# Moving the MLP's weight pieces inside longer buffers, by 16 to 448 bytes, with one raw buffer fewer

## The chip, the cores and the metric

The kernel runs on one core of one Trainium2 chip. The metric is the device time of one execution in microseconds, as the median of several runs; lower is better. The profile shows one execution on that core, with the engines TensorE (PE, its weight loads as PEld), VectorE (DVE), ScalarE (ACT), GpSimd (POOL) and the queue of SyncE (SP), which issues the transfers.

## The reference

One decoder layer on 256 tokens of width 2048, in float32. The input is normalised and multiplied by one wide matrix `w_in`; its columns feed a state-space group and an attention group with a token indexer. Their outputs are joined, multiplied by `w_out` and added to the input. Then comes the MLP, where most of the time lies:

```python
    x = x + jnp.concatenate([y_ssd, y_att], axis=-1) @ w_out      # w_out: 2048 x 2048

    u = rmsnorm(x, g_mlp) @ w_up                                  # w_up: 2048 x 8192
    return x + jnp.square(jax.nn.relu(u)) @ w_down                # w_down: 8192 x 2048
```

Every weight is read once, 204 MB in all, and every product is 256 rows high.

## The kernel before, in words

A float32 weight is split into a high part in TensorE's rounded float32 format and the rest, in the same format, and the activations likewise. A product is then three matrix multiplications: high by high, high by low, low by high. All of them add up in PSUM.

Weights come in **pieces** of 128 partitions by at most 1024 columns (4 KB a partition, 512 KB in all). The function `operands` makes one piece: SP issues its transfer into a buffer `raw` (L119), ACT copies it to `whi` with rounding (L122), DVE subtracts the two and writes `wlo` (L123). There are four buffers for `raw` (RB) and five each for `whi` and `wlo` (WB). A buffer is used again when its last reader is done: a `raw` when DVE has subtracted, a `whi` or `wlo` when TensorE is past its last matmul.

TensorE's order is written by hand. ACT's, DVE's and SP's is set by a scheduler that works with estimated times and priorities; pieces have a priority that places them 600 instructions ahead.

Two functions use pieces:

- `product` has the weights as the **moving** operand: two 512-column slices to a piece. The activations are the stationary operand, loaded 128 columns at a time (512 bytes a partition). Per slice and block of 128 rows there are three matmuls: L141 (high, high), L142 (the activations' low part), L143 (the weights' low part). The blocks of `w_in` named k, m0, m1, q0, q1, z0 and z1, the product with `w_out` and the MLP's `down` use it. The blocks m0 and m1 are 304 columns wide, the others 512.
- `product_t` has the weights as the **stationary** operand: eight 128-column slices to a piece. The moving operand is the activations, high and low side by side: 512 columns against the high weights (L181), 256 against the low ones (L182). The blocks qi and xbc of `w_in` and the MLP's `up` use it.

The MLP has four quarters q. `up(q)` makes eight units j of 256 columns of u (four pieces, 32 pairs of L181 and L182 each). `down(q)` makes four units j of 512 output columns (eight pieces, 96 matmuls each). The order is up(0), up(1), down(0), up(2), down(1), up(3), down(2), down(3). The very first unit of up(0) is multiplied ahead of the loop.

Where things stand in a partition's memory is fixed when the program is built. In bytes past a multiple of 512, the program of before has every `whi` and every `wlo` at 480 (its ten buffers are 4096 bytes apart), the activations `hx` and `x2x` at 32, and `uh`, `ul`, `yah`, `yal`, `ysh` and `ysl`, the stationary operands of `down` and of the product with `w_out`, at 224. Slices of 128 or 512 columns keep these remainders, because they are whole multiples of 512 bytes. In the blocks of 304 columns the second slice of a piece is 1216 bytes on, at 160.

Of the kernel before, what the change touches and what calls it, by code (L numbers as in the profile page):

```python
# [10 lines left out]
F32R = mybir.dt.float32r  # L11
# [5 lines left out]
P = 128  # L17
# [10 lines left out]
HP = 600  # L28
WARM = 9
WB = 5  # L30
RB = 4


Z0, XBC0, DT0, Q0, K0, V0, QI0, KI0, WI0, END = (
# [31 lines left out]
def hymba_kernel(ctx: ExitStack, tc: tile.TileContext, xn, xt, w_in, w_out, w_up, w_down, vcol, vrow, out):  # L66
# [3 lines left out]
    wts = ctx.enter_context(tc.tile_pool(name="wts", bufs=1))  # L70
# [24 lines left out]
    def step():  # L95
        for t in list(tasks):
            if isinstance(t[1], int) and t[1] > 0:
                t[1] -= 1
            elif not isinstance(t[1], str) or t[1] in done:
                advance(t)  # L100
# [6 lines left out]
        return vc[:, VC[name] + i:VC[name] + i + 1]  # L107


    def operands(src, n, load=None):  # L110

        with tc.high_priority(offset=HP):
            raw = wts.tile([P, n], F32, name="raw", tag="raw", bufs=RB)
            hi = wts.tile([P, n], F32R, name="whi", tag="whi", bufs=WB)
            lo = wts.tile([P, n], F32R, name="wlo", tag="wlo", bufs=WB)
            step = n if load is None else n // 2
            for i in range(0, n, step):
                s = slice(i, i + step)
                nc.sync.dma_start(raw[:, s], src[:, s])  # L119
                if load is not None:  # L120
                    load()
                nc.scalar.copy(hi[:, s], raw[:, s])  # L122
                nc.vector.tensor_tensor(lo[:, s], raw[:, s], hi[:, s].bitcast(F32), op=OP.subtract)  # L123
        return hi, lo

    def mp(name):
        return ps.tile([P, 512], F32, name=name, tag="mid")

    def accumulators():
        return [ps.tile([P, 512], F32, name="acc", tag="acc") for _ in range(2)]  # L130

    def product(src, n, left, load=None, tail=None):


        acc = accumulators()
        last = KT if tail is None else KT - 4

        def part(kt, out, b, wh, wl):
            s = slice(b * P, (b + 1) * P)
            ah, al = left(kt)  # L140
            nc.tensor.matmul(out, ah[:, s], wh, start=(kt == 0), stop=False)  # L141
            nc.tensor.matmul(out, al[:, s], wh, start=False, stop=False)  # L142
            nc.tensor.matmul(out, ah[:, s], wl, start=False, stop=(kt == KT - 1))  # L143

        kept = []
        halves = [(1, slice(0, n // 2)), (1, slice(n // 2, n))]
        if tail is not None:
            acc.append(mp("acc_t"))
        for kt in range(KT):
            if kt % 2 == 0:  # L150
                hi, lo = operands(src[kt // 2], 2 * n, load)
            w = slice(kt % 2 * n, kt % 2 * n + n)
            wh, wl = hi[:, w], lo[:, w]
            if kt < last:
                part(kt, acc[0][:, :n], 0, wh, wl)
                if tail is None:
                    part(kt, acc[1][:, :n], 1, wh, wl)
                else:
                    for i, (b, c) in enumerate(halves):
                        part(kt, acc[1 + i][:, c], b, wh[:, c], wl[:, c])  # L160
            else:
                kept.append((kt, wh, wl))
            step()
        if tail is not None:
            for i, (b, c) in enumerate([(0, slice(0, n))] + halves):
                for kt, wh, wl in kept:
                    part(kt, acc[i][:, c], b, wh[:, c], wl[:, c])
                tail(b, c, acc[i][:, c])
        return acc

    def product_t(src, right):

        acc = accumulators()
        for i in range(4):
            hi, lo = operands(src[i], 1024)
            c = i % 2
            for k in range(8):
                kt = 8 * (i // 2) + k
                x = right(kt)
                s = slice(k * P, (k + 1) * P)  # L180
                nc.tensor.matmul(acc[c], hi[:, s], x, start=(kt == 0), stop=False)  # L181
                nc.tensor.matmul(acc[c][:, T:], lo[:, s], x[:, :T], start=False, stop=(kt == KT - 1))  # L182
                if k % 4 == 3:
                    step()
        return acc

    def total(dst, acc):

        for c in range(2):
            nc.scalar.copy(dst[:, c, :], acc[c][:, T:])  # L190
            nc.vector.tensor_tensor(dst[:, c, :], acc[c][:, :T], dst[:, c, :], op=OP.add)
# [45 lines left out]
    for name, cols in IN_BLOCKS:  # L237
        n = sum(b - a for a, b in cols)
# [3 lines left out]
    def in_block(name, load=None):  # L242
        o, n = in_off[name]
        src = w_in[o:o + n * D].rearrange("(g p c) -> g p c", g=8, p=P)
        return product(src, n, h_left, load)

    def in_pair(name, i):
        o = in_off[name][0] + i * 256 * D
        return product_t(w_in[o:o + 256 * D].rearrange("(h p c) -> h p c", h=4, p=P), lambda kt: hx[:, kt, :])
# [436 lines left out]
    def run():  # L686
# [58 lines left out]
        for j in range(4):  # L745
            spawn(residual(j, product(w_out[j], 512, y_left)), f"res{j}")
# [4 lines left out]
    def x2(kt):  # L751
        if kt >= KT - 4:
            need("res3")
        return box[0][:, kt, :]

    first = product_t(w_up[0], x2)
    while tasks:
        step()
# [11 lines left out]
    def up(q):  # L770
        uh = mlp.tile([P, KT, T], F32R, name="uh")
        ul = mlp.tile([P, KT, T], F32R, name="ul")
        for j in range(8):
            r = mlp.tile([P, 2, T], F32, name="r")
            total(r, first if q + j == 0 else product_t(w_up[8 * q + j], x2))
            nc.vector.scalar_tensor_tensor(r, r, 0.0, r, op0=OP.max, op1=OP.mult)
            s = slice(2 * j, 2 * j + 2)
            nc.scalar.copy(uh[:, s, :], r)
            nc.vector.tensor_tensor(ul[:, s, :], r, uh[:, s, :].bitcast(F32), op=OP.subtract)
        return uh, ul  # L780

    def down(q, u):
        for j in range(4):

            def add(b, c, acc):
                c = slice(512 * j + c.start, 512 * j + c.stop)
                nc.vector.scalar_tensor_tensor(xr[:, b, c], acc, rs4[:, b:b + 1], xr[:, b, c], op0=OP.mult, op1=OP.add)
                if q == 3:
                    nc.sync.dma_start(out[b * P:(b + 1) * P, c], xr[:, b, c])

            end = q == 3 and j == 3
            acc = product(w_down[4 * q + j], 512, lambda kt: (u[0][:, kt, :], u[1][:, kt, :]), tail=add if end else None)
            for b in range(0 if end else NB):
                add(b, slice(0, 512), acc[b])

    u = [up(0)]
    for q in range(1, 4):
        u.append(up(q))
        down(q - 1, u[q - 1])
    down(3, u[3])  # L800


# [50 lines left out]
```

## Time and profile before

| | |
|---|---|
| time, median of 3 runs | 1112.91 us (1112.75 to 1113.02) |
| the profiled execution's own time | 1111.47 us |
| its span, first to last instruction | 1109.4 us |
| TensorE busy | 1100.4 us (99%) |
| TensorE's weight loads busy | 937.9 us (85%) |
| DVE busy | 692.4 us (62%) |
| ACT busy | 535.0 us (48%) |
| read from HBM | 204.29 MB, 186 GB/s over the span |

A busy TensorE is one with a matmul under way. Matmuls overlap, so the length of one says little. What counts is the distance from the start of one to the start of the next, which is read from the first and the last start in a stretch and the count between them. A wait of ACT or DVE costs something only where TensorE then waits for them.

### The profile page before, as it was taken

The numbers are of one execution on the slowest core, as the hardware profiler recorded it, in microseconds if no ns is written. First come the engines' busy times: TensorE is split into PE (matmuls) and PEld (weight loads), VectorE is DVE, ScalarE is ACT, GpSimd is POOL, SyncE is SP. The second block draws the span as 40 slices with busy tenths as digits, with TensorE's granted clock in tenths as the row PEclk, the third lists the DMA queues.
The fourth block names the chain that finished last, engine by engine and source line by source line (L and its number), as shares of the span: only waits on it lengthen the run. The fifth ranks groups of instructions, "written<-read, shape, count | busy, mean of one in ns | idle before, by whom it ended". The sixth has DMA issues, their size and how long they took to land.

```text
span 1109.4 us, 14959 instructions
## 1 busy us (share of the span) xinstructions
PE 1100.4 (99%) x5686; PEld 937.9 (85%) x5686; DVE 692.4 (62%) x976; ACT 535.0 (48%) x749; POOL 41.4 (4%) x41
## 2 busy tenths in 40 slices
PE   9999998999999999999999999999999999999998
PEld 7988887888888888888888888888888888888887
DVE  6886989667765565656565456565555565554443
ACT  7755645556765454444443334444434444333431
POOL 0010131112000000000000000000000000000000
PEclk9999999999999999999999999999999999999999
DMA  9855435644375555556656655655666556665662
GB/s 327 270 195 175 152 106 175 194 147 134 115 256 185 184 181 184 187 189 189 183 186 198 193 190 190 191 190 190 192 192 191 188 188 191 198 195 191 209 212 73
DMA packets 63735, 207.36 MB, mean 187 GB/s; under 512 B 7216, under 2 KB 11568, under 8 KB 63664
## 3 DMA queue, kind: packets, MB, share of 16 engines
q1 hardware_dynamic: 63520, 206.36, 58.1%
q8 instruction: 45, 0.74, 0.3%
q14 instruction: 26, 0.21, 0.1%
q10 hardware_dynamic: 144, 0.05, 0.0%
HBM read 204.29 MB, written 2.10 MB: 186 GB/s over the span
## 4 chain that ended last, share of the span: by engine, by line
PE 92%; DVE 4%; DMA 1%; issue 1%; ACT 1%; SPq 0%; POOL 0%; ACTq 0%; DVEq 0%
PE acc L181 27%; PE acc L141 16%; PE acc L142 16%; PE acc L143 16%; PE acc L182 14%; DVE wlo L123 1%; DVE bc L495 1%; PE ps_y L566 1%; DVE sc L459 1%; DMA xrow<-in_xn 1%; PE ps_sr L650 0%; PE ps_l L604 0%; PE ps_o L629 0%; ACT xrow L230 0%; DMA raw<-in_w_in 0%
## 5 line engine op out<-in xcount | busy, mean ns | idle before, releaser
L123 DVE TENSOR_TENSOR wlo<-raw,whi 128x1024 fp32r<-128x1024 f32 (+3 forms) x400 | 466.9, 1170 | 380.9 <-ACT whi L122 377.7
L122 ACT CAST whi<-raw 128x1024 fp32r<-128x1024 f32 (+3 forms) x400 | 400.5, 1004 | 497.4 <-PE acc L142 248.7
L181 PE MATMUL acc<-x2x,whi 128*128 128x512 f32 x1024 | 359.9, 395 | 0.0
L182 PE MATMUL acc<-x2x,wlo 128*128 128x256 f32 x1024 | 287.8, 281 | 0.0
L181 PEld LDWEIGHTS acc<-x2x,whi 128*128 128x128 f32 x1024 | 192.5, 188 | 45.4
L142 PE MATMUL acc<-whi,ul 128*128 128x512 f32 (+1 forms) x512 | 197.6, 386 | 0.0
L141 PE MATMUL acc<-whi,uh 128*128 128x512 f32 (+1 forms) x512 | 197.5, 386 | 0.0
L143 PE MATMUL acc<-wlo,uh 128*128 128x512 f32 (+1 forms) x512 | 197.5, 386 | 0.0
L182 PEld LDWEIGHTS acc<-x2x,wlo 128*128 128x128 f32 x1024 | 192.0, 188 | 0.1
L181 PE MATMUL acc<-hx,whi 128*128 128x512 f32 x320 | 114.0, 397 | 0.0
L141 PEld LDWEIGHTS acc<-whi,uh 128*128 128x128 f32 x512 | 96.1, 188 | 19.5
L143 PEld LDWEIGHTS acc<-wlo,uh 128*128 128x128 f32 x512 | 96.1, 188 | 19.5
L142 PEld LDWEIGHTS acc<-whi,ul 128*128 128x128 f32 x512 | 96.2, 188 | 19.2
L182 PE MATMUL acc<-hx,wlo 128*128 128x256 f32 x320 | 90.0, 281 | 0.0
L143 PE MATMUL acc<-wlo,hx 128*128 128x512 f32 (+1 forms) x224 | 83.0, 370 | 3.1 <-DVE wlo L123 3.1
L141 PE MATMUL acc<-whi,hx 128*128 128x512 f32 (+1 forms) x224 | 85.4, 381 | 0.1
L142 PE MATMUL acc<-whi,hx 128*128 128x512 f32 (+1 forms) x224 | 82.6, 369 | 0.0
L181 PEld LDWEIGHTS acc<-hx,whi 128*128 128x128 f32 x320 | 60.3, 188 | 13.5
L182 PEld LDWEIGHTS acc<-hx,wlo 128*128 128x128 f32 x320 | 60.1, 188 | 0.0
L143 PEld LDWEIGHTS acc<-wlo,hx 128*128 128x128 f32 x224 | 42.0, 187 | 12.0 <-DVE wlo L123 4.7
L141 PEld LDWEIGHTS acc<-whi,hx 128*128 128x128 f32 x224 | 42.2, 188 | 7.7 <-issue 0.7
L142 PEld LDWEIGHTS acc<-whi,hx 128*128 128x128 f32 x224 | 42.1, 188 | 7.4 <-issue 0.7
(224 smaller groups left out, 828.4 us busy)
## 6 DMA issues: line engine op xcount, KB each, us to landing
raw<-in_w_up SPq DMA_DIRECT2D x128, 512.0 KB, 3.7
raw<-in_w_down SPq DMA_DIRECT2D x128, 512.0 KB, 4.0
raw<-in_w_in SPq DMA_DIRECT2D x72, 512.0 KB, 3.6
raw<-in_w_out SPq DMA_DIRECT2D x32, 512.0 KB, 3.6
raw<-in_w_in SPq DMA_DIRECT2D x16, 256.0 KB, 4.2
raw<-in_w_in SPq DMA_DIRECT2D x16, 152.0 KB, 5.3
raw<-in_w_in SPq DMA_DIRECT2D x8, 304.0 KB, 2.9
xT<-in_xt SPq DMA_DIRECT2D x16, 128.0 KB, 4.1
```

The source lines that it names most:

```text
L122: nc.scalar.copy(hi[:, s], raw[:, s])
L123: nc.vector.tensor_tensor(lo[:, s], raw[:, s], hi[:, s].bitcast(F32), op=OP.subtract)
L141: nc.tensor.matmul(out, ah[:, s], wh, start=(kt == 0), stop=False)
L142: nc.tensor.matmul(out, al[:, s], wh, start=False, stop=False)
L143: nc.tensor.matmul(out, ah[:, s], wl, start=False, stop=(kt == KT - 1))
L181: nc.tensor.matmul(acc[c], hi[:, s], x, start=(kt == 0), stop=False)
L182: nc.tensor.matmul(acc[c][:, T:], lo[:, s], x[:, :T], start=False, stop=(kt == KT - 1))
L459: nc.vector.scalar_tensor_tensor(sc[:, :nk], rl[:, i, :nk], wis[:, b, h:h + 1], neg[:, T - nk:] if first else sc[:, :nk], op0=OP.mult, op1 ...
L495: nc.vector.scalar_tensor_tensor(o[:, j, :], pad[:, j, k:k + T], vcp("conv_w", 12 * k + ct), o[:, j, :], op0=OP.mult, op1=OP.add)
L566: nc.tensor.matmul(pt[:, 64 * i:64 * i + 64], m[i // 4][:, i % 4, :], xdt[:, c, 64 * h:64 * h + 64], start=True, stop=True)
```

## The change

Two things are edited. The buffers for `whi` and `wlo` get 128 more columns (512 bytes a partition), and in the MLP a piece is placed `shift` columns into its buffer. The shift comes from a table, by quarter and unit. For `up(q)`, unit j, it is entry j of row q; for `down(q)`, unit j, it is entry j + 1. All other pieces, and the first unit of up(0), are at shift 0. In bytes, the shifts of `up` are 64j for q = 0, 32j for q = 1, 16j for q = 2 and 64(7 - j) for q = 3; those of `down` are 64, 128, 192, 256 for q = 0; 32, 64, 96, 128 for q = 1; 16, 32, 48, 64 for q = 2; and 384, 320, 256, 192 for q = 3. And there are three buffers for `raw` instead of four.

A buffer is now 4608 bytes, nine times 512, and ten of them add 5120 bytes; the dropped `raw` gives back 4096. In the built program of the change `whi` and `wlo` still start at 480 past a multiple of 512 at shift 0, `x2x` still at 32, `uh` and `ul` still at 224. So the shifts are all that changes in these remainders.

```diff
-RB = 4
+RB = 3
+SPARE = 128
+
+
+SHIFTS = [[16 * j for j in range(8)], [8 * j for j in range(8)], [4 * j for j in range(8)], [16 * (7 - j) for j in range(8)]]
...
-    def operands(src, n, load=None):
+    def operands(src, n, load=None, shift=0):
 
         with tc.high_priority(offset=HP):
             raw = wts.tile([P, n], F32, name="raw", tag="raw", bufs=RB)
-            hi = wts.tile([P, n], F32R, name="whi", tag="whi", bufs=WB)
-            lo = wts.tile([P, n], F32R, name="wlo", tag="wlo", bufs=WB)
+            hi = wts.tile([P, n + SPARE], F32R, name="whi", tag="whi", bufs=WB)[:, shift:shift + n]
+            lo = wts.tile([P, n + SPARE], F32R, name="wlo", tag="wlo", bufs=WB)[:, shift:shift + n]
...
-    def product(src, n, left, load=None, tail=None):
+    def product(src, n, left, load=None, tail=None, shift=0):
...
-                hi, lo = operands(src[kt // 2], 2 * n, load)
+                hi, lo = operands(src[kt // 2], 2 * n, load, shift)
...
-    def product_t(src, right):
+    def product_t(src, right, shift=0):
 
         acc = accumulators()
         for i in range(4):
-            hi, lo = operands(src[i], 1024)
+            hi, lo = operands(src[i], 1024, None, shift)
...
-            total(r, first if q + j == 0 else product_t(w_up[8 * q + j], x2))
+            total(r, first if q + j == 0 else product_t(w_up[8 * q + j], x2, SHIFTS[q][j]))
...
-            acc = product(w_down[4 * q + j], 512, lambda kt: (u[0][:, kt, :], u[1][:, kt, :]), tail=add if end else None)
+            acc = product(w_down[4 * q + j], 512, lambda kt: (u[0][:, kt, :], u[1][:, kt, :]), tail=add if end else None,
+                          shift=SHIFTS[q][j + 1])
```

TensorE, POOL: the same instructions in the same order. On ACT, DVE and SP the scheduler moves some, since there are three `raw` buffers to plan with. The change adds four lines ahead of `operands`, so L119, L122 and L123 read L123, L126 and L127 there.

The first place is DVE at the end of block m0: the two subtractions of 304 columns are m0's last piece, its halves, and `rt_x` and `ry_x` are steps of a reciprocal root that DVE works out for the input's norm. Before:

```order
L281 TENSOR_SCALAR rt_x<-rt_x 128x2
L335 TENSOR_REDUCE s_361<-sq 128x4
L123 TENSOR_TENSOR wlo<-raw,whi 128x304 x2
L282 TENSOR_TENSOR ry_x<-rt_x,ry_x 128x2
L279 TENSOR_TENSOR rt_x<-ry_x 128x2
L280 TENSOR_TENSOR rt_x<-rt_x,rx_x 128x2
```

With the change:

```order
L285 TENSOR_SCALAR rt_x<-rt_x 128x2
L339 TENSOR_REDUCE s_361<-sq 128x4
L286 TENSOR_TENSOR ry_x<-rt_x,ry_x 128x2
L283 TENSOR_TENSOR rt_x<-ry_x 128x2
L127 TENSOR_TENSOR wlo<-raw,whi 128x304
L284 TENSOR_TENSOR rt_x<-rt_x,rx_x 128x2
L127 TENSOR_TENSOR wlo<-raw,whi 128x304
```

The first half now stands behind two steps of the root, the second behind three.

The second place is SP's queue at the same point of the program, where `vr` is a small table of constants. Before:

```order
L228 DMA xrow<-in_xn 128x2x512
L119 DMA raw<-in_w_in 128x304 x8
L290 DMA vr<-in_vrow 128x48
L119 DMA raw<-in_w_in 128x1024 x40
L119 DMA raw<-in_w_in 128x608 x8
```

With the change:

```order
L232 DMA xrow<-in_xn 128x2x512
L123 DMA raw<-in_w_in 128x304 x6
L294 DMA vr<-in_vrow 128x48
L123 DMA raw<-in_w_in 128x304 x2
L123 DMA raw<-in_w_in 128x1024 x40
L123 DMA raw<-in_w_in 128x608 x8
```

The last piece of block m0 (two halves) is now issued behind `vr`; the pieces keep their order among themselves.

## The prediction, made before the changed kernel was run

> **What bounds the kernel now.** I read the page first, then stretches of the span by stage, then the first and last start of TensorE's matmuls in single stages. TensorE is under way for all but 9 us, at the full granted clock, and carries 92% of the chain that ended last:
>
> ```profile
> PE 1100.4 (99%) x5686; PEld 937.9 (85%) x5686; DVE 692.4 (62%) x976; ACT 535.0 (48%) x749; POOL 41.4 (4%) x41
> PEclk9999999999999999999999999999999999999999
> PE 92%; DVE 4%; DMA 1%; issue 1%; ACT 1%; SPq 0%; POOL 0%; ACTq 0%; DVEq 0%
> ```
>
> So the time is made of the distance from one matmul to the next, times 4096 matmuls in the MLP. The next table has one row for each of: block k (L141 over `hx`), `down(0)` (L141 over `uh`), quarters 0 and 3 of `up` (L181), and block m0. Each gives the first and the last start and the count. The last two rows are weight loads.
>
> ```profile
> L141 PE MATMUL acc<-whi,hx x26: 394/394/394, 8.8 to 26.3; 128*128 128x512 f32 x26
> L141 PE MATMUL acc<-whi,uh x60: 389/389/389, 604.7 to 644.8; 128*128 128x512 f32 x60
> L181 PE MATMUL acc<-x2x,whi x185: 392/397/398, 454.9 to 519.9; 128*128 128x512 f32 x185
> L181 PE MATMUL acc<-x2x,whi x187: 392/392/396, 859.8 to 924.7; 128*128 128x512 f32 x187
> L141 PE MATMUL acc<-whi,hx x32: 298/302/303, 28.4 to 41.4; 128*128 128x304 f32 x32
> L141 PEld LDWEIGHTS acc<-whi,uh x59: 187/188/188, 605.2 to 644.6; 128*128 128x128 f32 x59
> L181 PEld LDWEIGHTS acc<-x2x,whi x184: 187/188/189, 455.1 to 519.8; 128*128 128x128 f32 x184
> ```
>
> L141 is every third matmul, so block k runs at 17.5/25/3 = 233.3 ns a matmul and `down` at 40.1/59/3 = 226.6. They are the same instructions on the same shapes at the same clock, and both are fed in time (one length for all, no idle time). What differs is which stationary operand they read: `hx` starts at 32 past a multiple of 512 bytes, `uh` at 224, with the weights at 480 in both. A pair of L181 and L182 takes 65.0/184 = 353.3 ns in quarter 0 and 64.9/186 = 348.9 in quarter 3, at equal starts; so there are also 4.4 ns a pair that the placement doesn't explain.
>
> **A working model of that distance**, an estimate from these rows alone. A weight load reads 512 bytes in 188 ns, 2.7 bytes/ns. It runs beside the matmul ahead of it, which reads 2048 bytes. Suppose that the matmul loses one step whenever its read passes the load's at the same place modulo 512 bytes (the five buffers lie multiples of 512 apart, and the one length in each row above shows no difference between them). Let a step be 233.3 - 226.6 = 6.7 ns, with two steps lost in `down` and three in block k. Then a matmul without loss takes 226.6 - 13.4 = 213.2 ns, 9.6 bytes/ns. The faster read gains 6.9 bytes/ns and laps the load every 512/6.9 = 74 ns, which is 188/74 = 2.5 times a load: two or three, by where the two start. Where loads follow each other without pause, as in `up` (two of 188 in 351 ns) and m0, only the mean counts. It gives 320/(1 - 6.7/74) = 352 ns for a pair of 768 columns and 126.7/0.91 = 139 for 304 columns. The rows say 349 to 353 and 13.0/31/3 = 139.8. So three shapes fit with one step.
>
> [...]
>
> **The change part by part.**
>
> *The shift in `down`.* It moves the weights' start and leaves `uh` and `ul`. The distance from the moving start to the stationary one, modulo 512, is 64 in block k (three steps) and 256 in `down` today (two). With the shift it is 256 less the shift: 192, 128, 64, 0 in q = 0; 224, 192, 160, 128 in q = 1; 240, 224, 208, 192 in q = 2; 384, 448, 0, 64 in q = 3. A mean of 2.5 says that about half of the circle costs three steps: a stretch of some 270 bytes that holds 64 and not 256. I put its end half-way, at 160, so it begins at 160 - 270 + 512 = 402. Slow are then 128, 64, 0, then 128, then 448, 0, 64: seven units of sixteen, with the unit at 160 on the edge and not counted. A unit has 96 matmuls, so 96 x 6.7 ns = 0.64 us, and seven are **+4.5 us**. Bounds within the model: with the end at just over 64, six units (0, 64, and all four of q = 3), +3.8; with the end just under 256, fourteen, +9.0. No unit can gain in it, since all have two steps today.
>
> *The shift in `up`.* Here the weights are what is loaded, without pause, so the mean should stay: **0**. Bounds are the two distances that rows show at one placement: all of the 512 pairs of one half at the other's value, 512 x 4.4 ns = 2.2 us to either side.
>
> *ACT and DVE write and read the shifted pieces.* In `down` both wait for buffers:
>
> ```profile
> L122 ACT CAST whi<-raw x23: 1056/1056/1061, 599.9 to 659.8; 128x1024 fp32r<-128x1024 f32 x23
>   PE acc L142: 38.3, 23
> L123 DVE TENSOR_TENSOR wlo<-raw,whi x22: 1224/1226/1226, 601.0 to 658.1; 128x1024 fp32r<-128x1024 f32 x22
>   ACT whi L122: 28.4, 19
> ```
>
> ACT is idle for 38.3 us of 60 until TensorE frees a buffer, DVE for 28.4 until ACT is done. Were each 0.3 us slower at some offset, it would still cost **0**; no row has another start to price it by. A piece lasts 12 x 226.6 = 2.72 us on TensorE; the cover is gone when ACT's 1.06 or DVE's 1.23 comes near that, and from there each 0.1 us a piece costs 0.1 us, 12.8 us over the 128 pieces of `down`.
>
> *Three raw buffers in the MLP.* The transfer of a piece now starts when the piece three ahead of it is subtracted. A turn is landing 4.0 + cast 1.06 + subtraction 1.23, 6.3 us with no gap, against 3 x 2.72 = 8.2 us that TensorE needs for three pieces (8.4 in `up`, with eight pairs a piece). So **0**, with 1.9 us to spare.
>
> ```profile
> raw<-in_w_down SPq DMA_DIRECT2D x128, 512.0 KB, 4.0
> raw<-in_w_in SPq DMA_DIRECT2D x16, 152.0 KB, 5.3
> 34.19 1.63 DVE L123 TENSOR_TENSOR wlo<-raw,whi 128x304 fp32r<-128x304 f32 x4
> 40.16 0.30 PE L141 MATMUL acc<-whi,hx 128*128 128x304 f32 x1
> 41.84 0.39 PE L181 MATMUL acc<-hx,whi 128*128 128x512 f32 x1
> ```
>
> *Three raw buffers ahead of it.* In m0 a piece lasts only 12 x 139.8 ns = 1.7 us, 5.0 for three, and its halves take 5.3 us to land. m0's last piece waits for the subtraction of the one three ahead, the first two of the four at 34.19, which end at about 35.05. It lands at 40.35, and its first half is cast and subtracted at 41.2. TensorE starts on that piece at 40.16 today, and reads `wlo` 0.3 us later: 0.75 us late, and the two steps of the root that now stand ahead add to it. The pieces of qi behind it come every 2.4 us against the 2.8 that TensorE takes for one, so the lag isn't passed on. Block m1 has the same width, but there DVE sets the pace already:
>
> ```profile
> PEld acc L143 <- DVE wlo L123: 4.3, 5, 2.0
> PE acc L143 <- DVE wlo L123: 3.1, 3, 1.8
> ACT whi L122 <- DMA raw<-in_w_in: 2.9, 4, 1.4
> ```
>
> (waits from 150 to 200 us: TensorE for DVE, and ACT for transfers in four places only). I take **+1.0 us** for both; bounds are 0, where DVE's own order hides it, and 2, with a like lag in m1.
>
> *SP.* The last piece of m0 goes behind `vr`, whose issue is one instruction of 0.4 us in a queue that waits for buffers at that point: inside the term above.
>
> *The sum.* The profiled execution took 1111.47 us itself, 2.07 around its span of 1109.4, and the median of the runs shown is 1112.91, 1.44 more. 4.5 + 0 + 1.0 = +5.5: 1117.0 beside the profiled one, **1118.4 us** beside the median.
>
> **The rivals.**
>
> *Offsets do nothing.* Then 233.3 against 226.6 comes from something else that block k has, such as `hx` holding high and low in one tile 1024 bytes apart while `uh` and `ul` are far apart. For it: `up` has two distances at one placement. Against it: the product with `w_out`, whose stationary operand starts at 224 too but has its two parts 8192 bytes apart in other tiles, runs at 10.2/15/3 = 226.7, as `down` does:
>
> ```profile
> L141 PE MATMUL acc<-whi,ysh x16: 389/389/389, 340.1 to 350.3; 128*128 128x512 f32 x16
> ```
>
> Time: 1112.9 + 1.0 = 1113.9. [...]
>
> *Faster: units whose weights start at a multiple of 64 bytes.* Every operand here starts at 32 past a multiple of 64. A step of 6.7 ns is 64 bytes at 9.6 bytes/ns, so a row of 2048 bytes may be read as 33 stretches of 64 where 32 would do. Then shifts of an odd multiple of 32 bytes save one step: in `down` three units (32 and 96 in q = 1, 32 in q = 2), 3 x 0.64 = 1.9 us; in `up`, if loads gain likewise, six units of 64 loads (q = 1, j odd; q = 2, j = 2 and 6), 6 x 64 x 6.7 = 2.6. Together -4.5, and +1.0 for the buffers: 1109.4. It decides if no other unit loses. Against it: hx and uh start alike modulo 64, and still differ by a step.
>
> *Three raw buffers starve TensorE.* The spare 1.9 us in the MLP holds for a landing of 4.0; in m0, m1 and the early 512-wide blocks it is short. If each of the 16 pieces of m0 and m1 came 0.25 us late, it would be +4: 1116.9, slower with no change in the matmuls' distance. Against it: five pieces of `whi` stand between ACT and TensorE.
>
> **How the numbers follow.** The forecast has 0.51, with a range of its own from 1116.7 (+3.8 + 0) to 1123.9 (+9.0 + 2); offsets that do nothing 0.28; the faster rival 0.14; starving 0.07. A difference under 0.2%, 2.2 us, can't be told from none here. Faster takes 0.13 of its rival, and 0.01 of the second. Same takes 0.20 of "nothing", 0.05 where losses and gains of the forecast cancel and 0.01 of the faster rival: 0.26. Slower is the rest: 0.46 of the forecast, 0.07 of "nothing" with a dearer m0 or `up` at its worse value, and 0.07 of starving: 0.60. Faster is 0.14. The range, 1110.5 to 1122.5, leaves out most of the faster rival (0.12) and the far end of the model (0.06).
>
> **What would show it.** In the profile after, one row of L141 for each unit of `down`: 233 ns a matmul in the seven units named, 226.6 in the rest. Equal distances in all sixteen make the offset rival right; distances of 220 at odd multiples of 32 bytes the faster one. `up` should stay from 348.9 to 353.3 a pair at every shift; a pair outside breaks "only the mean counts". Starving would be idle time of TensorE behind DVE L127 ahead of 60 us or in the MLP. The prediction fails if `down` goes under 226 or `up` under 347.

## The result, and the profile after

The changed kernel takes **1129.07 us** in the median (1126.94 to 1129.85, 4 runs) against 1112.97 (1112.75 to 1113.05): a ratio of 1.0142, with a 95% interval from 1.0124 to 1.0160. It is slower, by 16.1 us. The forecast was 1118.4, with a range from 1110.5 to 1122.5. The profiled execution took 1126.94, its span is 1124.8, and that is 15.4 us more than the profiled one of before. In what follows, one execution of the fourth experiment that took 2302.96 us, for a reason that isn't known, is left out of its numbers.

The page of the profile after (busy time, the granted clock in 40 slices, the chain of waits by engine) gives little away:

```profile
PE 1109.6 (99%) x5686; PEld 940.1 (84%) x5686; DVE 692.3 (62%) x976; ACT 533.8 (47%) x749; POOL 42.0 (4%) x41
PEclk9999999999999999999999999999999999999999
PE 90%; DVE 3%; DMA 3%; ACT 1%; issue 1%; SPq 0%; POOL 0%; ACTq 0%; DVEq 0%
```

TensorE is busy for 9.2 us more and idle for 6.2 more, and the chain has 3% of DMA where it had 1%. So two things happened. TensorE has the same instructions in the same order in both kernels, so each can be matched with itself, and the later start read off (start after less start before):

| at (us, in the kernel before) | 25 | 50 | 75 | 200 | 400 | 578 | 665 | 755 | 842 | 931 | end |
|---|---|---|---|---|---|---|---|---|---|---|---|
| delay (us) | 0.3 | 2.8 | 9.0 | 9.7 | 10.0 | 8.5 | 9.9 | 9.8 | 11.9 | 12.8 | 15.4 |
| what ends there | | | | | ahead of the MLP | up(0), up(1) | down(0) | up(2) | down(1) | up(3) | down(2), down(3) |

**10.0 us of the 15.4 arise before the MLP begins**, most of it in one place. In the MLP `up` gives back 0.7 (-1.5, -0.2, +0.9) and `down` costs 6.1 (1.4, 2.1, 2.6).

**The one place.** Waits from 40 to 70 us, before and after (us in total, times, the longest; line numbers are 4 higher after):

```profile
ACT whi L122 <- DMA raw<-in_w_in: 2.8, 5, 1.0
...
PE ps_ki L376 <- DVE kd L371: 0.5, 1, 0.5
```

```profile
ACT whi L126 <- DMA raw<-in_w_in: 10.0, 7, 3.8
...
PE ps_ki L380 <- DVE kd L375: 5.4, 1, 5.4
```

ACT now waits 10.0 us for weights, and TensorE stands still for 5.4 us in front of one transpose, the one of the index keys (`ps_ki`), until DVE has scaled them (`kd`). It waited 0.5 us there before, so the keys had no time in hand.

The keys are made from block m0. ACT moves m0's result out of PSUM (`sm`) and sums the squares (`kss`, done at the ACTIVATION_READ_ACCUMULATOR row below); DVE takes a reciprocal root of `kss` (`rx_ki` to `krs`) and scales the keys with it. None of this needs a weight of qi, but it stands between qi's pieces in the queues of ACT and DVE, and both timelines run in the order that the scheduler has set: after, `sm` at 50.81 behind a cast at 49.86, the root at 55.32 behind a subtraction at 54.18. They tell what was late (start, duration, instruction, idle time just before). Before:

```profile
43.23 1.06 ACT L122 CAST whi<-raw 128x1024 fp32r<-128x1024 f32 x1 [0.23 <-DMA raw<-in_w_in]
44.19 0.33 ACT L306 ACTIVATE sm<-acc,rstd 128x96 f32<-128x96 f32 x1
...
47.36 0.20 ACT L365 ACTIVATION_READ_ACCUMULATOR kj<-sm 128x1 f32 x1
```

```profile
46.55 1.23 DVE L123 TENSOR_TENSOR wlo<-raw,whi 128x1024 fp32r<-128x1024 f32 x1 [0.78 <-ACT whi L122]
47.69 0.16 DVE L273 TENSOR_SCALAR rx_ki<-kss 128x2 f32<-128x2 f32 x1
...
53.42 0.41 DVE L371 TENSOR_SCALAR kd<-sm,krs 128x64 f32<-128x64 f32 x2
```

After:

```profile
49.86 1.05 ACT L126 CAST whi<-raw 128x1024 fp32r<-128x1024 f32 x1 [3.79 <-DMA raw<-in_w_in]
50.81 0.34 ACT L310 ACTIVATE sm<-acc,rstd 128x96 f32<-128x96 f32 x1
...
54.19 0.21 ACT L369 ACTIVATION_READ_ACCUMULATOR kj<-sm 128x1 f32 x1
```

```profile
50.94 1.23 DVE L127 TENSOR_TENSOR wlo<-raw,whi 128x1024 fp32r<-128x1024 f32 x1 [3.62 <-ACT whi L126]
...
52.76 1.23 DVE L127 TENSOR_TENSOR wlo<-raw,whi 128x1024 fp32r<-128x1024 f32 x1
...
54.18 1.23 DVE L127 TENSOR_TENSOR wlo<-raw,whi 128x1024 fp32r<-128x1024 f32 x1
55.32 0.16 DVE L277 TENSOR_SCALAR rx_ki<-kss 128x2 f32<-128x2 f32 x1
...
61.15 0.57 DVE L375 TENSOR_SCALAR kd<-sm,krs 128x64 f32<-128x64 f32 x3
```

The cast ahead of `sm` is that of qi's fourth piece. That piece is issued at 44.7, when the piece three ahead of it is subtracted, and is itself subtracted at 52.2 (45.5 before): a turn of a buffer of 7.5 us. Its cast starts at 49.9 instead of 43.2, so `sm` is moved 6.6 us later (ACT was idle for 3.8 us ahead of that cast, and m0's last matmul starts at 42.9), and `kss` is complete at 54.4 instead of 47.6, 6.8 us later. On DVE the root stands behind subtractions of these pieces as well and starts at 55.3 instead of 47.7, 7.6 us later. So most of the lag came through ACT's queue, and DVE's added 0.8. The scheduler's order has a smaller part: on DVE it differs here too, not at the end of m0 alone, and the root now has six pieces of qi ahead of it where it had five. The fifth is done at 54.0, so this is 1.3 us at most. The transpose starts 8.3 us later than before: 0.9 of this arose at m0's fifth piece, 1.6 at qi's first, and 5.4 is the wait.

A second cost follows the first. Stretches of the span in the changed kernel (TensorE's busy time comes after the length, the granted clock stands third from the end):

```profile
56.00:58.00 2.00, 0.05 (x1) 0.00 (x0) 2.00 (x14) 0.91 (x2) 0.00 (x0) 1.00 0.92 264
58.00:60.00 2.00, 0.00 (x0) 0.00 (x0) 2.00 (x23) 0.92 (x2) 0.00 (x0) 1.00 0.81 213
60.00:61.00 1.00, 0.00 (x0) 0.00 (x0) 1.00 (x2) 0.91 (x1) 0.00 (x0) 0.97 0.76 258
61.00:62.00 1.00, 0.54 (x3) 0.41 (x3) 1.00 (x7) 0.41 (x2) 0.00 (x0) 0.50 0.39 160
62.00:64.00 2.00, 2.00 (x8) 1.71 (x8) 2.00 (x7) 0.00 (x0) 0.00 (x0) 0.50 0.80 252
64.00:66.00 2.00, 2.00 (x12) 1.75 (x12) 1.79 (x6) 0.02 (x1) 1.81 (x1) 0.91 0.46 117
```

After 5.4 us of standing still, TensorE goes on with a granted clock of 0.50 until about 64.4 us. That adds 1.1 us to the delay (7.9 to 9.0). In the fourth experiment the same clock followed waits of 1.5 and 0.8 us. The 0.7 us between 75 and 200 us come between 175 and 190, where the granted clock is at 0.50 for 3.4 us again; that place was not followed further.

**The units of `down`.** One row of L145 (every third matmul) for each of six units:

```profile
L145 PE MATMUL acc<-whi,uh x31: 392/392/392, 586.7 to 607.3; 128*128 128x512 f32 x31
L145 PE MATMUL acc<-whi,uh x32: 394/394/394, 631.0 to 652.7; 128*128 128x512 f32 x32
L145 PE MATMUL acc<-whi,uh x32: 388/389/395, 653.4 to 674.5; 128*128 128x512 f32 x32
L145 PE MATMUL acc<-whi,uh x32: 394/394/403, 808.7 to 830.4; 128*128 128x512 f32 x32
L145 PE MATMUL acc<-whi,uh x32: 393/395/397, 966.0 to 987.7; 128*128 128x512 f32 x32
L145 PE MATMUL acc<-whi,uh x32: 394/394/397, 1055.1 to 1076.4; 128*128 128x512 f32 x32
```

The distances (stationary start less moving start, modulo 512) are 192, 64, 0, 160, 224 and 448. The first and last starts give 228.9, 233.3, 226.9, 233.3, 233.3 and 229.0 ns a matmul. Taken modulo **256**, all units fall in line. Means over the unrounded starts:

| distance modulo 256 | 0 | 64 | 128 | 160 | 192 | 208 | 224 | 240 |
|---|---|---|---|---|---|---|---|---|
| `down`, ns a matmul | 226.7–227.2 | 233.3 | 232.3–233.4 | 233.5 | 228.9–229.0 | 233.3 | 233.2–233.3 | 231.8 |
| `up`, ns a pair | 346.5–346.8, or 353.2–353.6 | 352.8–353.3 | 350.6–351.2 | 351.3 | 348.8–349.1, or 353.0 | 349.6 | 346.7–346.8 | 353.0 |

(In `up` 16 and 48 gave 347, 32 gave 346.7 or 353.1, and 96 gave 346.8.) Before, the distance was 0 in all of `down` and 192 in all of `up`. So `down` started from its best value, and every unit but the two at 0 lost; `up` started from a middling one and got a mixture. Two units of `up`, at 0 and 64, and the two last of up(2), at 32 and 48 together:

```profile
L185 PE MATMUL acc<-x2x,whi x33: 392/392/395, 418.2 to 429.3; 128*128 128x512 f32 x33
L185 PE MATMUL acc<-x2x,whi x33: 392/397/398, 429.3 to 440.6; 128*128 128x512 f32 x33
L185 PE MATMUL acc<-x2x,whi x65: 392/392/397, 741.8 to 764.0; 128*128 128x512 f32 x65
```

11.1/32 = 347, 11.3/32 = 353 and 22.2/64 = 347 ns a pair. ACT and DVE in the shifted pieces of `down`, against 1056 and 1226 ns before:

```profile
L126 ACT CAST whi<-raw x22: 1047/1048/1055, 600.5 to 658.8; 128x1024 fp32r<-128x1024 f32 x22
  PE acc L146: 38.0, 22
```

```profile
L127 DVE TENSOR_TENSOR wlo<-raw,whi x23: 1224/1226/1227, 598.8 to 659.9; 128x1024 fp32r<-128x1024 f32 x23
```

### The profile page after: what moved, and what is told of

It is laid out like the page before. It is cut to its first block, busy times and chain, and to the rows that moved or that the text cites. A ratio compares the mean times of both kernels' runs of the same rounds, so it can differ in the third digit from the quotient of the medians.

```text
span 1124.8 us, 14957 instructions
## 1 busy us (share of the span) xinstructions
PE 1109.6 (99%) x5686; PEld 940.1 (84%) x5686; DVE 692.3 (62%) x976; ACT 533.8 (47%) x749; POOL 42.0 (4%) x41
## 4 chain that ended last, share of the span: by engine, by line
PE 90%; DVE 3%; DMA 3%; ACT 1%; issue 1%; SPq 0%; POOL 0%; ACTq 0%; DVEq 0%
PE acc L185 26%; PE acc L145 15%; PE acc L146 15%; PE acc L147 15%; PE acc L186 13%; DMA raw<-in_w_in 2%; DVE wlo L127 1%; ACT whi L126 1%; DMA raw<-in_w_out 1%; PE ps_y L570 1%; DMA xrow<-in_xn 1%; DVE sc L463 1%; DVE bc L499 0%; PE ps_sr L654 0%; PE ps_l L608 0%
## 5 line engine op out<-in xcount | busy, mean ns | idle before, releaser
L127 DVE TENSOR_TENSOR wlo<-raw,whi 128x1024 fp32r<-128x1024 f32 (+3 forms) x400 | 467.4, 1170 | 396.2 <-ACT whi L126 393.8
L126 ACT CAST whi<-raw 128x1024 fp32r<-128x1024 f32 (+3 forms) x400 | 399.2, 1000 | 524.6 <-PE acc L146 254.5
L145 PE MATMUL acc<-whi,uh 128*128 128x512 f32 (+1 forms) x512 | 199.5, 390 | 0.0
L145 PEld LDWEIGHTS acc<-whi,uh 128*128 128x128 f32 x512 | 96.1, 188 | 21.6
L145 PE MATMUL acc<-whi,hx 128*128 128x512 f32 (+1 forms) x224 | 86.4, 386 | 0.2 <-ACT whi L126 0.2
L145 PEld LDWEIGHTS acc<-whi,hx 128*128 128x128 f32 x224 | 42.8, 191 | 8.1 <-ACT whi L126 0.9
```

## The experiments

Each was timed in three rounds (the last in five) beside the kernel before on the same chip, whose median there was 1113.20, 1112.90 and 1112.66 us. All of them compute everything. They are numbered in this order, and some `-` lines are left out of the diffs. The profiled execution of before was a quick one, 1.4 us under its median; delays against it come out larger by about that than differences of medians do.

**1. Only the buffers: three for `raw`, no shift.**

```diff
-RB = 4
+RB = 3
```

> The kernel of before with three raw buffers instead of four and nothing else. Theory A (the two parts add up: the missing raw buffer costs about 10 us ahead of the MLP, the shifts about 5.5 us inside it): +9 to +11.5 us, TensorE waits about 5 us once for the index keys (ps_ki), the MLP from its first up matmul on is as long as before within 1 us. Rival B (the longer buffers and the shifts also cause the early loss, for instance by moving other tiles in memory): less than +4 us. Rival C (three buffers starve the MLP too): the MLP is longer by 3 us or more.

Measured: 1122.73 us, +9.5, ratio 1.0085 (1.0068 to 1.0102). The wait at the transpose is there (waits, 40 to 70 us), and the clock is down after it (a window):

```profile
PE ps_ki L376 <- DVE kd L371: 4.7, 1, 4.7
```

```profile
60.00:64.00 4.00, 2.39 (x8) 1.96 (x9) 4.00 (x15) 1.12 (x2) 0.00 (x0) 0.50 0.64 230
64.00:70.00 6.00, 6.00 (x29) 5.20 (x28) 4.51 (x8) 1.05 (x1) 5.54 (x4) 0.76 0.27 92
```

`down` runs at 40.1/59/3 = 226.6 ns, as before:

```profile
L141 PE MATMUL acc<-whi,uh x60: 389/389/389, 604.9 to 645.0; 128*128 128x512 f32 x60
```

The delay is 11.0 us at 325 us and 11.0 at the end, without a change in between. So theory A holds, B and C fall: three buffers cost ahead of the MLP alone, and far more than the +1.0 there. The buffer comes with the scheduler's new order, which is the changed kernel's on DVE; no run has the one without the other.

**2. Only the shifts: four buffers for `raw`, 64 spare columns instead of 128, shifts modulo 64 columns.** There was no room for 128. This gives each unit the change's shift modulo 256 bytes, not modulo 512.

```diff
+SPARE = 64
+SHIFTS = [[16 * j % 64 for j in range(8)], [8 * j for j in range(8)], [4 * j for j in range(8)], [16 * (7 - j) % 64 for j in range(8)]]
```

> Four raw buffers; buffers longer by 64 columns (256 bytes) instead of 128; each shift of the table is taken modulo 256 bytes. The buffers now start at 480 and at 224 past a multiple of 512 in turn. Theory A with a period of 256 bytes: +4.5 to +7 us, all of it in the MLP, with the same distance in each unit as in the changed kernel (227 ns where the distance of the two starts is 0 modulo 256, 229 at 192, 232 to 233.5 at 64, 96, 128, 160, 208, 224 and 240). Rival (the period is 512 bytes, or the place in memory matters): the distances within a unit differ from piece to piece, and the unit means do not repeat. Rival (shifts cost nothing by themselves): within 2 us of before.

Measured: 1118.65, +5.5, ratio 1.0047 (1.0032 to 1.0062). Each unit of `up` and `down` runs at the pace of the changed kernel's unit to about 0.1 ns a matmul or pair, although its distance modulo 512 is often another. The MLP as a whole gets 5.4 us longer in both. So the period is 256 bytes. 9.5 + 5.5 = 15.0 of the change's 16.1: the parts add up within the intervals of the runs.

**3. One shift for `up`: 32 bytes in all its units, none in `down`, four buffers.**

```diff
+    first = product_t(w_up[0], x2, 8)
...
+            total(r, first if q + j == 0 else product_t(w_up[8 * q + j], x2, 8))
```

> Four raw buffers, buffers longer by 64 columns, one constant shift of 32 bytes (8 columns) for the pieces of up and none for down. Theory A (the start of the weight load against the moving operand sets the pair's distance): the pairs of up, 353.3 ns in quarters 0 and 1 and 348.9 in 2 and 3 before, run at 348.6 throughout as in the two units with this start in the changed kernel; down stays at 226.7; together -2 to -3 us. Rival (up has two states whatever the start, which a unit only falls into): the pairs stay between 348.6 and 355 with some quarters at 353 or more, and the time is within 2 us of before.

Measured: **1108.28, -4.9**, ratio 0.9955 (0.9940 to 0.9970): faster than both kernels. The distance is 224 in all of `up`. Quarters 0 and 3:

```profile
L184 PE MATMUL acc<-x2x,whi x189: 390/390/390, 454.7 to 519.9; 128*128 128x512 f32 x189
L184 PE MATMUL acc<-x2x,whi x189: 390/390/390, 859.8 to 925.0; 128*128 128x512 f32 x189
```

65.2/188 = 346.8 ns a pair in both, where before had 353.3 and 348.9. 512 x 6.5 + 512 x 2.1 ns = 4.4 us. The gain is larger than the expected 2 to 3 us, because the expectation's 348.6 is another measure than its 353.3 (see the fifth experiment). What a pair takes in `up` isn't a mean that the placement leaves alone.

**4. Three buffers, and the transpose of the keys asked for nine steps later.**

```diff
-RB = 4
+RB = 3
...
-        yield 7
+        yield 16
         pt = mp("ps_ki")
```

> Three raw buffers, no shifts; TensorE takes up the transposes of the index keys (ps_ki) nine steps of its order later (16 instead of 7). Theory D (most of the early loss is one wait of TensorE for the index keys on VectorE, whose queue holds them behind subtractions that came late): the wait of 5.4 us is gone or under 1 us, and the time is +3 to +5 us over before instead of +9 to +11.5. Rival (the early weights themselves come too late, and the wait for the keys only hides that): the same loss shows as waits for the weights' subtraction or cast in blocks qi and xbc, and the time stays over +8 us.

Measured: 1116.92 in the median of five, +3.7, ratio 1.0032 (1.0019 to 1.0044), so 5.8 us under three buffers alone. The wait at the transpose is gone: that one wait and what it drew behind it made about three fifths of the loss, as theory D has it. That VectorE's queue is what held the keys was not tested by this run; its root starts at 56.7 here, again 0.9 us after `kss` is complete on ACT. Of what is left, 1.6 us arise at m0's fifth piece, and the rest between 43 and 50 us, where qi starts. Waits from 40 to 70 us:

```profile
PE acc L181 <- ACT whi L122: 1.5, 1, 1.5
...
PE acc L182 <- DVE wlo L123: 0.8, 1, 0.8
```

and windows there:

```profile
46.00:47.00 1.00, 0.34 (x2) 0.34 (x3) 0.94 (x2) 0.79 (x2) 0.00 (x0) 0.88 0.01 4
47.00:48.00 1.00, 1.00 (x4) 0.84 (x4) 0.97 (x2) 0.89 (x1) 0.00 (x0) 0.50 0.47 127
48.00:50.00 2.00, 2.00 (x8) 1.68 (x7) 1.14 (x1) 0.00 (x0) 0.00 (x0) 0.50 0.88 272
50.00:52.00 2.00, 2.00 (x13) 1.78 (x12) 0.00 (x0) 0.73 (x1) 0.00 (x0) 0.96 0.87 311
```

TensorE waits 1.5 and 0.8 us for qi's first piece, one matmul apart, and the granted clock then is at 0.50 again, from 47 to 50 us, for another 1.6 us of delay (4.6 to 6.2). The delay is 6.0 us from 190 us on.

**5. The activations moved, the weights left: `hx` 192 bytes on, `x2x` 32 bytes behind that.** If the distance is what counts, block k and its like should gain, and `up` as with its own shift.

```diff
+    keep.tile([P, 48], F32, name="pad_a")
-    hx = keep.tile([P, KT, 2 * T], F32R, name="hx")
+    hx = keep.tile([P, KT * 2 * T + 64], F32R, name="hx", tag="hx")[:, :KT * 2 * T].rearrange("p (k t) -> p k t", k=KT)
+    keep.tile([P, 16], F32, name="pad_b")
...
+                x2x = keep.tile([P, KT * 2 * T + 64], F32R, name="x2x", tag="hx")
+                box.append(x2x[:, 8:8 + KT * 2 * T].rearrange("p (k t) -> p k t", k=KT))
```

> The weights stay where they were, with four raw buffers; the activations move instead. hx starts 192 bytes later, at the same place modulo 256 as the weights (distance 0), and x2x starts 32 bytes behind hx's new start (distance 224, as in e3_up32). Theory F (only the distance modulo 256 bytes counts, whichever operand is moved): the 480 matmuls of blocks k, q0, q1, z0 and z1 go from 233.3 ns to 226.7 (480 x 6.6 = -3.2 us), pairs of L181 and L182 in up stay at 348.4 in all four quarters (about -4.9 as in e3_up32): 1105 us, 0.5 to 0.7% under before. Theory G (what helped in e3_up32 is where the weights start, not the distance): up stays at 349 to 355 a pair, blocks of 512 columns stay at 233: 1113 us. Blocks qi and xbc, now at distance 0, may run at either of the two paces that 0 has shown, which is 1.5 us to either side.

Measured: 1107.13, -5.8, ratio 0.9950 (0.9933 to 0.9966). Block k, and quarter 3 of `up`:

```profile
L141 PE MATMUL acc<-whi,hx x20: 389/389/389, 14.0 to 26.9; 128*128 128x512 f32 x20
L181 PE MATMUL acc<-x2x,whi x188: 390/390/390, 859.8 to 924.7; 128*128 128x512 f32 x188
```

12.9/19/3 = 226.3 (226.7 from the unrounded starts), where before had 233.3 at distance 64, and 64.9/187 = 347. Theory F holds for these paces, G falls. The time is 2 us over the expected 1105, in part because the blocks q0, q1, z0 and z1, where TensorE's matmuls are interrupted, reach 227.9 to 229.3 ns in the mean (distances over 300 ns not counted; 233.3 to 233.4 before), and not 226.7. (The 348.4 a pair in the expectation is twice the mean distance between the starts of one unit, which begins and ends inside a pair; from pair to pair it is 346.7.)

**6. All of `down` at distance 160.**

```diff
+                          shift=24)
```

> Four raw buffers; every piece of down 96 bytes into its buffer (distance 160 modulo 256), up as before. Theory F (modulo 256): all 16 units of down at 233.5 ns a matmul, 1536 x 6.8 ns = +10.4 us, 1123.5 us. Theory of the prediction (modulo 512, distance 160 on the edge, and no other mechanism): 226.6 or 233.3, 0 or +10.2. Theory H (what slows a unit is that neighbouring units have different offsets, not the offset itself): 226.7 throughout, 1113 us.

Measured: 1123.30, +10.4, ratio 1.0093 (1.0078 to 1.0108), as F said to 0.2 us. 64.4/92/3 = 233.3 ns, and the same in every unit but the last, which is cut into parts and was not read:

```profile
L144 PE MATMUL acc<-whi,uh x93: 399/399/399, 602.1 to 666.5; 128*128 128x512 f32 x93
```

That it meets F so closely is partly luck: the matmuls of `down` account for 9.7 us, and quarter 3 of `up`, whose operands weren't touched, runs at 353.4 ns a pair instead of 348.9, which is 1.1 us. So the start of the pieces of `down` alone is worth about 10 us here, and H falls: neighbours with different offsets aren't needed for it. The prediction's circle of 512 bytes, with 160 on its edge, isn't ruled out by this run but by the second experiment.

**7. Both operands of `down` 32 bytes on.**

```diff
+        uh = mlp.tile([P, KT * T + 64], F32R, name="uh")[:, 8:8 + KT * T].rearrange("p (k t) -> p k t", k=KT)
+        ul = mlp.tile([P, KT * T + 64], F32R, name="ul")[:, 8:8 + KT * T].rearrange("p (k t) -> p k t", k=KT)
...
+                          shift=8)
```

> Four raw buffers; in down the weights and uh and ul all start 32 bytes later, so that their distance stays 0 while each start is another; up's weights as before. Theory F (only the distance counts): 226.7 ns a matmul in all units of down, no change, 1113 us. Theory G (the weights' own start counts, which at 32 bytes gave 228.9 in after): 228.9, 1536 x 2.2 ns = +3.4 us, 1116.4 us. That the own start of both counts would show as any other distance.

Measured: 1115.33, +2.4, ratio 1.0021 (1.0011 to 1.0030). The time is between the two theories, and the rows say why: `down` keeps 64.6/95/3 = 226.7, so F holds for it. The loss is in `up`, whose operands weren't touched:

```profile
L144 PE MATMUL acc<-whi,uh x96: 389/389/389, 601.7 to 666.3; 128*128 128x512 f32 x96
L184 PE MATMUL acc<-x2x,whi x185: 392/397/398, 859.7 to 924.7; 128*128 128x512 f32 x185
```

65.0/184 = 353.3 ns a pair in quarters 2 and 3, where before had 348.9 there and 353.3 only in quarters 0 and 1. 512 x 4.4 ns = 2.3 us. In the sixth experiment, with the same buffers, quarter 2 had 348.9 and quarter 3 353.4. So at distance 192 a pair has two paces. Quarters that stood at 192 throughout kept one of them (before, 353.2 to 353.5 in the units of quarters 0 and 1 behind the first, 348.8 to 349.1 in those of 2 and 3), and here it was the other one in two quarters, with only `down` changed, which runs just ahead of them.

**8. Everything at its best distance: 0 where the weights are moved, 224 where they are loaded, in qi and xbc too.**

```diff
+    keep.tile([P, 16], F32, name="pad_a")
...
-    jp = keep.tile([P, P], I32, name="jp")
+    jp = mid.tile([P, P], I32, name="jp", **u2)
...
-    def product_t(src, right):
+    def product_t(src, right, shift=56):
```

(with 64 spare columns; `jp` makes room, and every operand then starts at 32 modulo 256.)

> Four raw buffers. All operands start at 32 modulo 256 bytes, and the pieces of product_t, in up and also in blocks qi and xbc, stand 224 bytes into their buffers: distance 0 wherever the weights are moved in 512 columns (k, q0, q1, z0, z1, w_out, down), 224 wherever they are loaded. Theory F (the distance modulo 256 decides, and a pair at 224 takes 346.7 ns from start to start, in every place): blocks of 512 columns at 226.7 (-3.2 us), 1024 pairs of up -4.5 us, 320 pairs of qi and xbc from 351 to 353 to 346.7, -1.5 to -2.0 us where TensorE isn't waiting there: 1104 us, 0.7 to 0.9% under before, and 1 to 2 us under e5_place. Rival I (qi and xbc are set by casts, subtractions and small matmuls in between, so their pairs' pace doesn't show): as e5_place, 1106 to 1107 us. A pair of up at 353 or a 512-column matmul at 233 would break F.

Measured: **1105.46, -7.2**, ratio 0.9929 (0.9916 to 0.9943), the best of all, where 1104 was expected. Block k at 226.7 ns; `up` at (924.6 - 859.8)/187 = 346.5, and 346.7 in all units of all quarters:

```profile
L144 PE MATMUL acc<-whi,hx x23: 389/389/389, 11.8 to 26.8; 128*128 128x512 f32 x23
L184 PE MATMUL acc<-x2x,whi x188: 390/390/390, 859.8 to 924.6; 128*128 128x512 f32 x188
```

Against the fifth experiment, it gains 1.4 us of span, 1.05 of them between 75 and 175 us, where the 320 pairs of qi and xbc go from about 351 to 347 ns: F again, and rival I falls.

## Why the prediction was wrong

The direction was right; the size was 16.1 us and not 5.5. Most of what is missing is in one term.

*Three raw buffers ahead of the MLP, +1.0 (0 to 2): the term that failed.* Alone it costs 9.5 us. The prediction priced one wait of TensorE for a late piece, m0's last, and then ended the matter with "The pieces of qi behind it come every 2.4 us against the 2.8 that TensorE takes for one, so the lag isn't passed on". A wait of that size did come, though at m0's fifth piece (0.9 us) and not at its last, and a second one at qi's first (1.6 us). From there to the transpose the delay stays at 2.8 us, so for qi's later pieces the sentence held. The step that failed is to take this for the whole lag. A turn of a buffer took 7.5 us (from one subtraction to the other, 44.7 to 52.2), not the 6.3 that had been added up for the MLP. And the queues of ACT and DVE hold more than pieces: what TensorE asked for next was not a piece but `ps_ki`, whose source `sm` stood on ACT behind the late cast of qi's fourth piece, and whose root stood on DVE behind late subtractions. The dearer part of a lag was at the instruction queued behind it: 5.4 us of waiting, and 1.1 us of slow clock after it. Neither was in the sum.

*Three raw buffers in the MLP, 0: right,* with the delay unchanged over 700 us in the first experiment.

*The shift in `down`, +4.5 (3.8 to 9.0): about right in size, by a wrong map.* Measured is +6.1. The step of 6.7 ns is real, and the range of paces, 226.7 to 233.5, is the one that the rows of before showed. But the lap was taken as 512 bytes, from the weight load's length; the pace repeats after 256 (second experiment), and that a lap makes it isn't shown. By 512, `down` stood half-way round from 0 and the units at 64, 128, 448 and 0 were to be slow. In fact `down` stood at the best place, 0 modulo 256. Of the seven units named, the two at 0 are fast, the one at 448 loses 2.3 ns only, and three of the four at 64 and 128 are slow (the fourth, the last of all, is cut into parts and was not read). The units at 160, 208, 224, 240 and 384 lose 5 to 7 ns each and weren't named. "The five buffers lie multiples of 512 apart" couldn't tell 512 from 256, and block k's 64 against `down`'s 256 couldn't either. The model also has no place for 192 being nearly as good as 0 with slow units on both sides. Its 213.2 ns for a matmul without loss was never seen: no stage of 512-column matmuls with a load for each ran under 226.6. That the model met the rows of three shapes was luck, and so, in part, was the size.

*The shift in `up`, 0 (±2.2): the sum was right (-0.7), its reason wrong.* "Only the mean counts" falls: a pair takes 346.7 to 353.6 by the distance, a step of 6.6 to 6.9 ns there too, and the mark set for failure, a pair under 347, was met. The 4.4 ns that the prediction left unexplained between two quarters at one placement was the sign that paces, not means, set it.

*ACT and DVE on shifted pieces, 0: right.* 1048 and 1226 ns against 1056 and 1226, with ACT idle for 38.0 us against 38.3.

*The rivals.* "Offsets do nothing" falls with the second experiment: one instruction took 226.7 or 233.3 ns by the load's start relative to the matmul's. Where the two get in each other's way, no run shows. "Units at a multiple of 64 bytes" falls as a rule: the unit of `down` at 224, whose weights start at a multiple of 512, is slow, and in `up` a shift of 96 bytes gave 353.1 ns in one unit and 346.7 in another. "Three raw buffers starve TensorE" came nearest, with the right sign to look for, idle time ahead of 60 us. It had 0.07 and +4, because it spread a quarter of a microsecond over 16 pieces instead of looking for what else waits in the queues of ACT and DVE.

## What to carry to other kernels

When a buffer is taken away from a ring, follow the lag past the first late piece, and past the ring: list what stands behind it in the queue of every engine that handles the pieces, find who needs that first and how much time it has in hand, and price that wait and the slow clock after it (5.4 and 1.1 us here). Where a matmul and a weight load overlap, the distance of their starts in memory can be a tuning parameter of its own: here a matmul of 512 columns took 226.7 to 233.5 ns by it, and a pair of `up` 346.7 to 353.6. Compare stages that run the same instruction at different paces, move one operand by a few tens of bytes, and read the pace from first and last starts. An offset table that varies by unit averages good and bad places; constants chosen from the paces that such a table shows were worth 4.9 us here (one shift, in `up`) to 7.2 us (all operands placed).

## What the hardware showed that wasn't expected

- The pace of 512-column matmuls, each with its own 128-column weight load, depends on the two operands' starts modulo 256 bytes: 226.7 to 227.2 ns at distance 0, 228.9 at 192, 231.8 to 233.5 at the others tried. It is the distance, not either start, that decides here: 226.7 in block k with the activations moved to distance 0 (fifth experiment), 226.7 in `down` with both operands moved by 32 bytes (seventh), 233.3 with the weights alone moved by 96 (sixth). Why 256 and why these places stays open.
- The pace is a rhythm that locks. In block k of the fifth experiment, after a disturbed start, the distances between starts go 224, 231, 236, 228, 233, 231, 226 ns and then stay at 227, 227, 226; the same run of distances stands at the start of `down(2)` in the kernel before, from 931.2 us. Pairs of `up` have two such rhythms at distances 0, 32 and 192 (346.7 or 353.3, 348.9 or 353.3), kept for long stretches (353.2 to 353.5 over fifteen units in a row in the kernel before); what chooses between them wasn't found. At 224 only 346.7 was seen, in every kernel that had it (346.5 to 347 in the rows above, of the changed kernel and experiments three, five and eight).
- The clock was halved for about 3.4 us in the changed kernel (0.97, 0.50, 0.50, 0.91 in the windows above add up to that), and for about twice as long in the first experiment (0.50 over 4 us and 0.76 over 6). TensorE had been waiting there, for 5.4 us and for 4.7, and in the fourth experiment for 1.5 and 0.8 us with one matmul between them. What sets it isn't shown: in the kernel before, TensorE stood still for 3.1 of the 8 us from 172 to 180, in waits of at most 1.8, and the granted clock was 1.00 there and up to 190.
